# The second layer's residual and two weight roundings change from GpSimd to VectorE

## The chip, the cores and the metric

The kernel runs on one core of a Trainium2 chip. The metric is the device time of one execution in microseconds (us). The engines are TensorE (PE: matmuls and transposes), VectorE (DVE), ScalarE (ACT), GpSimd (POOL) and SyncE (SP, which issues most DMAs). Each engine works through its own list of instructions in order, and an instruction waits on semaphores for what the other engines have to finish first. About 0.2% (2.3 us) is what a measurement of this kernel can tell from no change.

## The reference, cut to what matters

256 latent tokens and 256 context tokens of width 1024 go through a block of two layers (layer A: windowed attention; layer B: neighbourhood attention with a bias), then through a second block (dilated attention and a convolution, then a mixture of 32 experts). All is float32. The change touches the seam between the layers and the end of layer B:

```python
for i in range(DEPTH):                       # DEPTH = 2
    u = h * (1.0 + scale[:, None, :]) + shift[:, None, :]
    uc = hc * (1.0 + scale_c) + shift_c
    ...
    y, yc = mixer(u, uc, w_in, w_out, ...)
    h = layer_norm(DEEPNORM_ALPHA * h + gate[:, None, :] * y, ln_g[i], ln_b[i])
```

`layer_norm` is (x - mean) / deviation, times `ln_g`, plus `ln_b`. The kernel needs the normalized latents twice: as `u` for layer B's projections, and times `ln_g` plus `ln_b` (both multiplied by ALPHA beforehand) as the residual `h1` that is added to layer B's output much later.

## The kernel before, in words

**Products from pairs.** A float32 product is made from three TensorE products: each operand is split into a high half (`hi`, rounded by ScalarE) and a low half (`lo` = value - `hi`). For weights this is `wsplit` (L157 to L177): ScalarE casts 128x2048 in two pieces of 128x1024 (L170), and the subtraction (L175) is shared: the first `cut` of eight rows of 256 go to VectorE in pieces of up to four rows, the others to GpSimd in one piece. `cut` is 5 here, so VectorE gets 128x1024 and 128x256 of each chunk of 256 columns and GpSimd 128x768. For the input of layer B it is `to_u` (L655 to L673): TensorE transposes the tokens (L664), ScalarE makes scaled and shifted `ubhi` (L667), VectorE the same value `uf` (L671), and `ublo` is their difference (L673), on GpSimd for the context tokens and on VectorE for the latents. These differences are the tap roundings of the change's name.

**Between the layers.** `out_a` multiplies layer A's output with four chunks of 256 columns of its weight, adds it to the tokens (`xt`), gathers their statistics, and after the last chunk (`c == 3`) normalizes them in place (L653) and calls `to_u`, first for the context (t = 2, 3), then for the latents (t = 0, 1). Then come the four operations of the residual, on GpSimd: `xt` times `lng` (L723) and plus `lnb` (L724), 128x1024 each. `lng`, `lnb` and `xt` lie in a pool, `o1`, that ends there; the rooms of layer B take its place, so whatever is first written there waits for the last reader.

**Layer B.** For each of four groups G of heads: K into `KS` (`k_stack`: ScalarE casts at L742, VectorE differences at L744), V (ScalarE copies at L794, one for the context, one for the latents), Q (L729 to L735), the gate, then two attentions (m = 0, 1): scores (L835), bias and maximum on VectorE (L839), exponential on ScalarE (L278), division on VectorE (L284), transposes (L843), values (L849), gate (`og`, L852). The projections accumulate in three PSUM banks that all go by the name `mm` and are used in turn. Ahead of the last attention (G = 3, m = 1) the kernel splits weight chunks of layer B's output and of the next block's input; chunks 34 and 35 lie in the rooms of `ubhi` and `ublo`, which have no further use, and `cut = 0` gives their low halves wholly to GpSimd, 128x2048 each. After it come the output product (`osum`, L757) and its statistics (L867).

**Order.** A scheduler lists the instructions of each engine; it works by its own estimate of durations, and keeps the source's order only inside `tc.manual_schedule` for the engines named there. The line numbers after the change are those of before plus three to four, so L742 and L794 become L746 and L798, L839 becomes L841.

Of the kernel before, what the change touches and what calls it, by code (L numbers as in the profile page):

```python
# [13 lines left out]
OP = mybir.AluOpType  # L14
# [6 lines left out]
KT = 8  # L21
# [40 lines left out]
class Net:  # L62
# [621 lines left out]
    def out_a(self, ubp, ogp):  # L684
        tc, nc, d = self.tc, self.nc, self.d
        gr = self.row[0]
        self.ubhi = ubp.tile([P, KT, 512], F32R, name="ubhi")
        self.ublo = ubp.tile([P, KT, 512], F32R, name="ublo")
        sh, sc = self.mod["a", 0], self.mod["a", 1]
        fm = ubp.tile([P, 40], F32, name="fma")  # L690
        nc.sync.dma_start(fm, d["fmv"][:, :40])
        self.gn1 = fm[:, 32:40]
        ab = [self.mod_ab(ubp, fm[:, 0:8], fm[:, 16:24], sc[:, r], sh[:, r], f"mb{r}") for r in range(2)]
        with tc.tile_pool(name="o1", bufs=1, side="right") as o1:
            gates = [self.row_tile(o1, gr[0], "gate0"), self.gates[1]]
            self.xt[0] = o1.tile([P, 2, D], F32, name="xt")
            nc.scalar.dma_start(self.xt[0], d["xtok"][0:2].rearrange("t p d -> p t d"))
            xt = [self.xt[t // 2][:, t % 2, :] for t in range(4)]
            lng = self.row_tile(o1, d["lnrow"][0], "lng")
            lnb = self.row_tile(o1, d["lnrow"][1], "lnb")  # L700
            for r in (lng, lnb):
                nc.gpsimd.tensor_scalar(r, r, ALPHA, 0.0, op0=OP.mult, op1=OP.add)
            st = [o1.tile([P, 4, 6], F32, name=f"st{t}") for t in range(4)]
            ws = dict(enumerate(self.wo))
            for c, ts in ((0, (2, 3)), (1, (2, 3)), (0, (0, 1)), (1, (0, 1)), (2, (2, 3)), (3, (2, 3)), (2, (0, 1)), (3, (0, 1))):
                if c not in ws:
                    ws[c] = self.split("wa_out", c)
                cs = slice(c * 256, c * 256 + 256)
                for t in ts:
                    s = slice(t * P, t * P + P)  # L710
                    if c < 2 and t > 1:
                        y = self.yo[c][:, t - 2]
                        self.mm3(y, self.oparts, ws[c], s, slice(0, 256), range(AOK, KT), 1)
                    else:
                        y = self.ps.tile([P, 256], F32, name="mm", bufs=3)
                        self.mm3(y, self.oparts, ws[c], s, slice(0, 256))
                    self.ln_part(y, gates[t // 2][:, cs], xt[t][:, cs], xt[t][:, cs], st[t], c)
                    if c == 3:
                        self.ln_norm(xt[t], st[t])
                        if t % 2:  # L720
                            self.to_u([xt[t - 1], xt[t]], *ab[t // 2], self.ubhi, self.ublo, P * (t - 1), o1, own=0 if t > 1 else 2)
            for t in range(2):
                nc.gpsimd.tensor_tensor(self.h1[:, t, :], xt[t], lng, op=OP.mult)  # L723
                nc.gpsimd.tensor_tensor(self.h1[:, t, :], self.h1[:, t, :], lnb, op=OP.add)  # L724

    def q_dup(self, ps, qf, QD, scale=0.125):

# [18 lines left out]
    def layer_b(self, ubp):  # L746
        tc, nc, d = self.tc, self.nc, self.d
        u = (self.ubhi, self.ublo)
        lat, ctx, allt = slice(0, 256), slice(256, 512), slice(0, 512)
        with tc.tile_pool(name="b1", bufs=1, side="right") as b1:  # L750
# [3 lines left out]
            def osum(n, last=False):  # L754

                if not last:
                    nc.tensor.matmul(yo[n].rearrange("p i c -> p (i c)"), self.ident, self.h1[:, n // 2, n % 2 * 512:n % 2 * 512 + 512],  # L757
                                     start=True, stop=False, skip_group_check=True)
                for i in range(2):
                    self.mm3(yo[n][:, i], (oghi, oglo), wo[n % 2 * 2 + i], slice(n // 2 * P, n // 2 * P + P), slice(0, 256),  # L760
                             range(BOK, KT) if last else range(BOK), int(last))
# [5 lines left out]
            with tc.tile_pool(name="b2", bufs=1, side="right", reuse_waits="tile") as b2:  # L767
# [6 lines left out]
                for G in range(4):  # L774
# [14 lines left out]
                    for t2 in (1, 0):  # L789
                        ps = self.ps.tile([P, 2, 256], F32, name="mm", bufs=3)  # L790
                        for i in range(2):
                            t = 2 * t2 + i
# [14 lines left out]
                    for m in range(2):  # L807
                        self.filler(f"B{G}{m}")
                        if G == 3 and m == 1:
                            for n, t, b in (("whi", "KS", 4), ("wlo", "vacc", 2)):  # L810
                                self.place[n, 32] = Halves(*(b2.tile([P, 4, 256], F32R, name=t, bufs=b) for _ in range(2)))
                                self.place[n, 33] = Halves(*(self.sp.tile([P, 4, 256], F32R, name="slab", bufs=4) for _ in range(2)))
                            wo = [self.split("wb_out", c) for c in range(2)]
                            self.wsplit(34)
                            wo += self.wsp[32:34]
                            for i, n in ((34, "ubhi"), (35, "ublo")):
                                room = ubp.tile([P, KT, 512], F32R, name=n)
                                self.place["whi", i], self.place["wlo", i] = (room[:, :, j:j + 256] for j in (0, 256))
                            self.cut = 0
                            self.wsplit(36)  # L820
                            self.wn += 2
                            yo = [self.ps.tile([P, 2, 256], F32, name="mm", bufs=3) for _ in range(3)]
                            for n in range(3):
                                osum(n)
                        j = 2 * G + m
                        PT = [None, None]
                        for s in range(2):
                            h = 2 * j + s
                            bt = bias[h % 2]
                            nc.sync.dma_start(bt[:, :, :256], d["bias"][h].rearrange("t p c -> p t c"))  # L830
                            PT[s] = b2.tile([P, 4, 256], F32, name="PT", bufs=3)
                            for qt in range(2):
                                S = self.ps.tile([P, 512], F32, name="s", bufs=2)
                                for part in range(2):
                                    nc.tensor.matmul(S, QD[:, part, s, m, qt * P:qt * P + P], KS[m][:, s, :],  # L835
                                                     start=part == 0, stop=part == 1)
                                st = b2.tile([P, 512], F32, name="st", bufs=4)
                                nm = self.sm.tile([P, 1], F32, name="nm", bufs=6)
                                nc.vector.tensor_tensor_reduce(st, S, bt[:, qt, :], -1.0, BIG, OP.add, OP.min, nm)  # L839
                                self.softmax(st, 512, nm, 0)  # L840
                                pt = self.ps.tile([P, 4, P], F32, name="t", bufs=2)  # L841
                                for kt in range(4):
                                    nc.tensor.transpose(pt[:, kt, :], st[:, kt * P:kt * P + P], self.ident)  # L843
                                nc.scalar.copy(PT[s][:, :, qt * P:qt * P + P], pt)
                        O = self.ps.tile([P, 256], F32, name="o", bufs=1)
                        for kt in range(4):
                            for s in range(2):
                                hh = 2 * m + s
                                nc.tensor.matmul(O[64 * s:64 * s + 64, :], V[:, kt, hh * 64:hh * 64 + 64],  # L849
                                                 PT[s][:, kt, :], start=kt == 0, stop=kt == 3)  # L850
                        og = b2.tile([P, 256], F32, name="og", bufs=1)
                        nc.vector.tensor_tensor(og, O, sg[:, m], op=OP.mult)  # L852
                        nc.scalar.copy(oghi[:, j, :], og)
                        nc.gpsimd.tensor_tensor(oglo[:, j, :], og, oghi[:, j, :].bitcast(F32), op=OP.subtract)
            yo.append(self.ps.tile([P, 2, 256], F32, name="s", bufs=2))
            osum(3)
            with ExitStack() as es:
                b3 = es.enter_context(tc.tile_pool(name="b3", bufs=1, side="right", reuse_waits="tile"))
                lng = self.row_tile(b3, d["lnrow"][2], "lng")
                lnb = self.row_tile(b3, d["lnrow"][3], "lnb")  # L860
# [3 lines left out]
                for n in range(4):  # L864
                    osum(n, True)
                    t, c = divmod(n, 2)
# [832 lines left out]
```

## Time and profile before

| | |
|---|---|
| time, median of 3 runs | 1162.41 us (1161.33 to 1163.54) |
| profiled execution | 1162.07 us |
| its span on the core | 1160.3 us, granted clock 0.979 |
| PE busy | 1072.9 us (92%) |
| DVE busy | 673.6 us (58%) |
| ACT busy | 399.7 us (34%) |
| POOL busy | 144.9 us (12%) |
| DMA | 320.82 MB, mean 276 GB/s |

A share of busy time is a mean over stages that differ. From about 700 us on the experts run behind their weight stream; before that the projections and attentions run, and it is there that the change lies: at 305 to 345 us (end of `out_a`, start of layer B) and 517 to 547 us (last attention). The span is what the records cover; the profiled execution's own time is 1.8 us longer.

### The profile page before, as it was taken

Reading aid. Unit: us, or ns where it says so; the run is one execution under the profiler, and the core shown is the slowest. Engines: PE = TensorE matmul, PEld = TensorE weight load, DVE = VectorE, ACT = ScalarE, POOL = GpSimd, SP = SyncE. Lnnn points to the kernel's source line nnn. Section 1 sums busy time; section 2 is a strip of 40 time slices with the busy share of each in tenths; the row PEclk is TensorE's granted clock in tenths of the full one; section 3 lists DMA queues with packets and bytes.
Section 4 is the critical chain, followed back from the end, with each engine's and each line's share of the span. In section 5 each row is a group of like instructions: output and inputs, shape, how many; then the busy total and the mean of one; then the engine's idle time right before and its main releaser. Section 6 shows DMA issues by size and latency. Waiting matters only on the chain. (4 is left out here: it accounts for less than half of the span.)

```text
span 1160.3 us, 17034 instructions
## 1 busy us (share of the span) xinstructions
PE 1072.9 (92%) x6498; PEld 721.9 (62%) x6499; DVE 673.6 (58%) x1484; ACT 399.7 (34%) x791; POOL 144.9 (12%) x159
## 2 busy tenths in 40 slices
PE   6999999898979999997699898999999998989996
PEld 5777676667978888885689684443434343434432
DVE  3486566886989999895899864332323232322213
ACT  2265462761245645564346652111111010101112
POOL 0141122112442312143200000000000000000000
PEclk9999999999989999999799899999999999999999
DMA  9644528304338887344364787999999999999994
GB/s 364 250 140 152 200 94 285 112 19 141 127 123 310 305 278 264 124 152 149 107 242 154 292 342 273 417 421 420 421 419 422 421 420 421 420 421 421 421 420 173
DMA packets 58840, 320.82 MB, mean 276 GB/s; under 512 B 7001, under 2 KB 11777, under 8 KB 27522
## 3 DMA queue, kind: packets, MB, share of 16 engines
q1 hardware_dynamic: 58338, 318.58, 70.8%
q8 instruction: 53, 0.87, 0.3%
q10 hardware_dynamic: 416, 1.10, 0.3%
q14 instruction: 33, 0.27, 0.1%
HBM read 318.58 MB, written 1.07 MB: 275 GB/s over the span
## 5 line engine op out<-in xcount | busy, mean ns | idle before, releaser
L1433 PE MATMUL U<-ew,XT 128*64 128x512 f32 x512 | 120.8, 595 | 11.9 <-DMA ew<-wu 11.1
L1433 PE MATMUL G<-ew,XT 128*64 128x512 f32 x512 | 117.9, 596 | 4.8 <-DMA ew<-wg 4.7
L175 DVE TENSOR_TENSOR wlo<-raw,whi 128x1024 fp32r<-128x1024 f32 x84 | 100.4, 1218 | 22.4 <-ACT whi L170 22.3
L170 ACT CAST whi<-raw 128x1024 fp32r<-128x1024 f32 x84 | 84.0, 1049 | 82.8 <-PE mm L200 56.2
L1433 PEld LDWEIGHTS U<-ew,XT 128*64 128x64 f32 x512 | 39.4, 137 | 89.0 <-issue 65.3
L175 POOL TENSOR_TENSOR wlo<-raw,whi 128x768 fp32r<-128x768 f32 x32 | 68.3, 2135 | 187.9 <-ACT whi L170 181.7
L1433 PEld LDWEIGHTS G<-ew,XT 128*64 128x64 f32 x512 | 38.7, 137 | 77.5 <-issue 64.8
L278 ACT ACTIVATE st<-st,nm 128x513 f32<-128x513 f32 (+2 forms) x96 | 62.5, 654 | 56.3 <-DVE nm L839 36.2
L1535 DVE SCALAR_TENSOR_TENSOR eth<-eth,U 128x512 f32<-128x512 f32 x16 | 11.0, 688 | 108.8 <-PE U L1433 108.8
L200 PE MATMUL mm<-ublo,whi 128*128 128x256 f32 (+1 forms) x208 | 65.9, 317 | 4.6 <-DVE ublo L673 4.4
L200 PE MATMUL mm<-ubhi,wlo 128*128 128x256 f32 (+1 forms) x208 | 65.5, 315 | 1.3 <-DVE wlo L175 1.3
L228 DVE SCALAR_TENSOR_TENSOR vacc<-slab,stm,vacc 128x1024 f32<-128x1024 f32 x42 | 65.6, 1563 | 0.3
L200 PE MATMUL mm<-ubhi,whi 128*128 128x256 f32 (+1 forms) x208 | 65.4, 316 | 0.0
L1523 DVE SCALAR_TENSOR_TENSOR eth<-eth,G 128x512 f32<-128x512 f32 x16 | 11.0, 688 | 89.2 <-ACT eth L1522 89.2
L1441 ACT COPY hT<-x 128x512 f32<-128x512 f32 x15 | 8.8, 588 | 135.9 <-PE x L1439 135.9
L1452 PE MATMUL Y<-ew,hT 128*64 128x512 f32 x240 | 54.8, 598 | 0.0
L1452 PE MATMUL x<-ew,hT 128*64 128x512 f32 x240 | 54.5, 593 | 0.0
L200 PE MATMUL mm<-uhi,whi 128*128 128x512 f32 x128 | 51.9, 405 | 0.0
L284 DVE TENSOR_SCALAR st<-st,l 128x512 f32<-128x512 f32 (+1 forms) x96 | 50.8, 543 | 1.7
L200 PE MATMUL mm<-ulo,whi 128*128 128x512 f32 x128 | 51.5, 402 | 0.0
L200 PE MATMUL mm<-uhi,wlo 128*128 128x512 f32 x128 | 51.0, 399 | 0.0
L1347 POOL MEMSET ew<- 1x128 f32 x1 | 0.2, 195 | 378.5 <-DMA ew<-wu 378.5
(502 smaller groups left out, 2603.6 us busy)
## 6 DMA issues: line engine op xcount, KB each, us to landing
ew<-wg SPq DMA_DIRECT2D x64, 1024.0 KB, 19.8
ew<-wu SPq DMA_DIRECT2D x64, 1024.0 KB, 19.8
ew<-wd SPq DMA_DIRECT2D x63, 1024.0 KB, 19.8
slab<-wmod SPq DMA_DIRECT2D x48, 512.0 KB, 5.1
slab<-wada SPq DMA_DIRECT2D x32, 512.0 KB, 5.0
raw<-wb_in SPq DMA_DIRECT2D x16, 1024.0 KB, 5.0
raw<-wa_in SPq DMA_DIRECT2D x10, 1024.0 KB, 8.6
raw<-wc_in SPq DMA_DIRECT2D x10, 1024.0 KB, 4.9
```

The lines of the kernel that those rows point to most:

```text
L170: nc.scalar.copy(hi[:, k:k + self.piece[0]], raw[:, k:k + self.piece[0]])
L175: e.tensor_tensor(lo[:, k:to], raw[:, k:to], hi[:, k:to].bitcast(F32), op=OP.subtract)
L200: nc.tensor.matmul(out, a[x][:, k, sa], b[y][:, k, sb], start=(i == 0 and n == 0), stop=(i == len(ks) - 1 and n == 2))
L228: nc.vector.scalar_tensor_tensor(acc, slab, s, acc, op0=OP.mult, op1=OP.add)
L278: nc.scalar.activation(st[:, :width + extra], st[:, :width + extra], AF.Exp, bias=nm, scale=-1.0, accum_out=l[:, 0:1])
L284: nc.vector.tensor_scalar(st[:, :width], st[:, :width], l[:, 1:2], None, op0=OP.mult)
L1347: nc.gpsimd.memset(t[0:1, D:D + P], 1.0)
L1433: nc.tensor.matmul(o[64 * s:64 * s + 64, :], XT[p][k][:, 64 * s:64 * s + 64], self.ew[m, p, k // 4 * 2 + s][:, k % 4, :], start=k == 0, st ...
L1441: nc.scalar.copy(hT, pt)
L1452: nc.tensor.matmul(Y[64 * s:64 * s + 64, :], hT[:, f, 64 * s:64 * s + 64], w, start=f == 0, stop=f == 3)
L1523: nc.vector.scalar_tensor_tensor(th, th, 1.0, G, op0=OP.add, op1=OP.mult)
L1535: nc.vector.scalar_tensor_tensor(th, th, 0.5, U, op0=OP.mult, op1=OP.mult)
```

## The change

The residual moves to VectorE behind `to_u`, and from the last weight chunk of the latents on VectorE keeps the source's order. The low halves of chunks 34 and 35 move from GpSimd, ahead of the last attention in the source, to VectorE in pieces of four rows (`cut = KT`, KT = 8), behind it in the source.

```diff
@@ out_a
+                if c == 3 and 0 in ts:
+                    held = tc.manual_schedule(engines={mybir.EngineType.DVE})
+                    held.__enter__()
                 for t in ts:
...
             for t in range(2):
-                nc.gpsimd.tensor_tensor(self.h1[:, t, :], xt[t], lng, op=OP.mult)
-                nc.gpsimd.tensor_tensor(self.h1[:, t, :], self.h1[:, t, :], lnb, op=OP.add)
+                nc.vector.tensor_tensor(self.h1[:, t, :], xt[t], lng, op=OP.mult)
+                nc.vector.tensor_tensor(self.h1[:, t, :], self.h1[:, t, :], lnb, op=OP.add)
+            held.__exit__(None, None, None)
@@ layer_b
                                 self.place["whi", i], self.place["wlo", i] = (room[:, :, j:j + 256] for j in (0, 256))
-                            self.cut = 0
-                            self.wsplit(36)
                             self.wn += 2
...
                         nc.gpsimd.tensor_tensor(oglo[:, j, :], og, oghi[:, j, :].bitcast(F32), op=OP.subtract)
+            self.cut = KT
+            self.wsplit(36)
             yo.append(self.ps.tile([P, 2, 256], F32, name="s", bufs=2))
```

On VectorE at the end of `out_a`, of the change: the last of `to_u`, the residual (`h`, now L726 and L727), the low half of the Q chunk (`wlo_3416`), and the first sums of a modulation vector (`vacc`).

```order
L671 TENSOR_SCALAR uf<-s,mb_a,mb_c 128x256
L673 TENSOR_TENSOR ublo<-uf,ubhi 128x256
L726 TENSOR_TENSOR h<-xt,lng 128x1024
L727 TENSOR_TENSOR h<-h,lnb 128x1024
L726 TENSOR_TENSOR h<-xt,lng 128x1024
L175 TENSOR_TENSOR wlo_3416<-raw_2923,whi_3415 128x1024
L175 TENSOR_TENSOR wlo_3416<-raw_2923,whi_3415 128x256
L727 TENSOR_TENSOR h<-h,lnb 128x1024
L226 TENSOR_SCALAR vacc<-slab,stm 128x1024
```

Before, L226 followed directly on the last L673; the second L727 now stands six instructions behind it.

On ScalarE at the same place: `ubhi` of the latents, then K's casts, V's copies and the high half of the next chunk.

```order
 L667 ACTIVATE ubhi<-s,mb_c,mb_a 128x256 x2
-L794 ACTIVATE V<-mm 128x512
-L742 CAST KS<-mm 64x512 x2
-L170 CAST whi_3412<-raw_2923 128x1024 x2
-L742 CAST KS<-mm 64x512 x2
-L794 ACTIVATE V<-mm 128x512
-L170 CAST whi_3521<-raw_3301 128x1024 x2
...
+L170 CAST whi_3415<-raw_2923 128x1024 x2
+L746 CAST KS<-mm 64x512 x4
+L798 ACTIVATE V<-mm 128x512 x2
+L170 CAST whi_3524<-raw_3304 128x1024 x2
```

V's first copy (the context's) stood ahead of K's casts and now stands behind all four. The first `KS` lies where `lng` and `lnb` were, so its cast waits for the residual's last reader: L724 on GpSimd before, the second L727 on VectorE now. On TensorE the V product of the latents waits for V's first copy in both, since the copy frees its PSUM bank; the V product of the context stands ahead of the transposes of the latents' second tile now, and was shared out around both before.

On VectorE in the last attention, of the change (before, the rows are the same without the two L175 of `ubhi` and the two of `ublo`, and each L284 of the end follows its own RECIPROCAL):

```order
L284 TENSOR_SCALAR st<-st,l 128x512 x2
L175 TENSOR_TENSOR ubhi<-raw_5399,ubhi 128x4x256 x2
L841 ISA st,nm<-s,bias_3283 128x512
L841 ISA nm 128x1
L841 ISA st,nm<-s,bias_3283 128x512
L841 ISA nm 128x1
L175 TENSOR_TENSOR ublo<-raw_5609,ublo 128x4x256
L841 ISA st,nm<-s,bias_3284 128x512
L841 ISA nm 128x1
L175 TENSOR_TENSOR ublo<-raw_5609,ublo 128x4x256
L841 ISA st,nm<-s,bias_3284 128x512
```

So the scheduler puts the four pieces into the last attention, between its bias operations, though the source has them behind it. GpSimd has neither the residual nor a piece of 128x2048 any more.

## Rows read from the trace of the kernel before

**Rows 1.** Busy time by stretch: stretch, length, then each engine's busy us, PEclk, DMA share, GB/s
```profile
400.00:450.00 50.00, 49.55 (x340) 40.91 (x341) 46.08 (x70) 25.00 (x47) 11.45 (x8) 1.00 0.85 286
...
700.00:1150.00 450.00, 427.81 (x2050) 184.35 (x2051) 125.71 (x298) 61.32 (x109) 0.20 (x1) 1.00 0.97 402
```

**Rows 2.** Timeline of VectorE at the end of out_a: start, us, what, [idle before <-releaser]
```profile
317.35 2.90 DVE L653 TENSOR_SCALAR xt<-xt,mv,rs_y 128x1024 f32<-128x1024 f32 x1
...
322.80 2.48 DVE L673 TENSOR_TENSOR ublo<-uf,ubhi 128x256 fp32r<-128x256 f32 x1
...
328.83 0.53 DVE L671 TENSOR_SCALAR uf<-t,mb_a,mb_c 128x256 f32<-128x256 f32 x1
329.28 0.41 DVE L673 TENSOR_TENSOR ublo<-uf,ubhi 128x256 fp32r<-128x256 f32 x1
329.61 0.99 DVE L671 TENSOR_SCALAR uf<-s,mb_a,mb_c 128x256 f32<-128x256 f32 x2
...
331.52 0.74 DVE L226 TENSOR_SCALAR vacc<-slab,stm 128x1024 f32<-128x1024 f32 x1
```

**Rows 3.** Timeline of GpSimd, the residual of before
```profile
317.32 2.38 POOL L723 TENSOR_TENSOR h<-xt,lng 128x1024 f32<-128x1024 f32 x1 [2.59 <-DVE rs_y L634]
...
322.65 4.85 POOL L724 TENSOR_TENSOR h<-h,lnb 128x1024 f32<-128x1024 f32 x2
```

**Rows 4.** Timeline of TensorE, from K's product of the latents to the first attention
```profile
325.33 0.39 PE L200 MATMUL mm<-ublo,whi 128*128 128x256 f32 x1 [3.23 <-DVE ublo L673]
...
327.84 0.58 PE L200 MATMUL mm<-ublo,whi 128*128 128x256 f32 x1 [1.13 <-DVE ublo L673]
...
334.76 0.28 PE L200 MATMUL mm<-whi,ubhi 128*128 128x256 f32 x1
...
340.45 0.28 PE L200 MATMUL mm<-ubhi,whi 128*128 128x256 f32 x1
...
347.32 0.39 PE L200 MATMUL mm<-ubhi,wlo 128*128 128x256 f32 x1 [0.78 <-DVE wlo L175]
...
355.32 0.73 PE L835 MATMUL s<-KS,QD 128*128 128x512 f32 x2 [0.59 <-DVE QD L735]
```

**Rows 5.** Busy time by stretch around K's product of the latents (columns as in rows 1)
```profile
326.00:328.00 2.00, 0.87 (x5) 0.57 (x4) 2.00 (x3) 0.00 (x0) 2.00 (x3) 0.50 0.00 0
...
332.00:334.00 2.00, 2.00 (x17) 2.00 (x16) 1.93 (x3) 0.00 (x0) 0.00 (x0) 0.87 0.37 61
```

**Rows 6.** Timeline of ScalarE: V's copy of the context, K's casts, V's copy of the latents
```profile
324.39 0.63 ACT L794 ACTIVATE V<-mm 128x512 f32<-128x512 f32 x1
334.77 1.18 ACT L742 CAST KS<-mm 64x512 fp32r<-64x512 f32 x2 [9.75 <-PE mm L200]
...
340.65 0.60 ACT L794 ACTIVATE V<-mm 128x512 f32<-128x512 f32 x1 [1.48 <-PE mm L200]
```

**Rows 7.** Timeline of VectorE: two inputs of 128x1024, alone and beside GpSimd's L175
```profile
337.46 1.23 DVE L175 TENSOR_TENSOR wlo<-raw,whi 128x1024 fp32r<-128x1024 f32 x1
338.60 2.86 DVE L228 SCALAR_TENSOR_TENSOR vacc<-slab,stm,vacc 128x1024 f32<-128x1024 f32 x1
```

**Rows 8.** Timeline of GpSimd in the last attention
```profile
521.11 4.77 POOL L175 TENSOR_TENSOR ubhi<-raw,ubhi 128x2048 fp32r<-128x2048 f32 x1 [0.50 <-ACT ubhi L170]
```

**Rows 9.** Timeline of VectorE in the last attention
```profile
521.01 5.16 DVE L284 TENSOR_SCALAR st<-st,l 128x512 f32<-128x512 f32 x2
...
529.00 0.69 DVE L839 CUSTOM_DVE_ANT_0 st<-s,bias 128x512 f32<-128x512 f32 x1 [1.62 <-PE s L835]
...
533.56 0.49 DVE L284 TENSOR_SCALAR st<-st,l 128x512 f32<-128x512 f32 x1
```

**Rows 10.** Timeline of ScalarE in the last attention
```profile
525.90 2.00 ACT L170 CAST ublo<-raw 128x1024 fp32r<-128x1024 f32 x2 [3.91 <-DMA raw<-wc_in]
```

**Rows 11.** Timeline of TensorE in the last attention
```profile
526.31 0.63 PE L843 MATMUL t<-ident,st 128*128 128x128 f32 x4 [3.36 <-DVE st L284]
...
529.75 1.48 PE L757 MATMUL s<-h,ident 128*128 128x512 f32 x2
```

## The prediction

> **What bounds the kernel now.** I read the busy time by stretch first. From 700 us on the DMA engines are busy 97% of the time, and the experts run behind their weight stream; ahead of it, TensorE is busy 49.55 of 50 us between 400 and 450 [rows 1]. So TensorE sets the pace of layer B, and the stream begins behind the work that TensorE paces: a microsecond that TensorE loses at 305 to 345 us, or in the last attention, moves all that follows. The share of VectorE in that stretch, 46.08 of 50, says that it runs close behind and can't take much more.
>
> Then I read TensorE's timeline for its idle time at the two places of the change. At the end of `out_a` it waits 3.23 and 1.13 us for `ublo` (L673) on VectorE [rows 4]. VectorE is late there because its own instructions are long: one L653 takes 2.90 us and one L673 takes 2.48 [rows 2], while GpSimd works on the residual from 317.32 and again from 322.65 to 327.5 [rows 3]; an undisturbed L673 takes 0.41. Behind these waits the granted clock is 0.50 from 326 on and still 0.87 in 332 to 334 [rows 5], so 1.2 GHz from 327.84 to about 332.5, 4.7 us in which 2.3 us are lost. In the last attention TensorE waits 3.36 us for L284 [rows 11], two of which take 5.16 us [rows 9] beside GpSimd's piece of 128x2048, 4.77 us [rows 8].
>
> **The residual: what is given back.** With GpSimd quiet, `to_u` runs undisturbed: L671 and L673 follow each other every 0.78 us (328.83 to 329.61) [rows 2]. But the V product of the context now stands ahead of the transposes of the second tile. The first tile is normalized at about 317.2 (the next L653 starts at 317.35 [rows 2]); its transposes need 0.8 us (estimated), V's 48 matmuls 5.7 (as the V product of the latents takes from 334.76 to 340.45 [rows 4]). So the second transposes start near 323.7, VectorE's eight pairs near 324, and `to_u` ends at 324 + 8 x 0.78 = 330.2 instead of 331.5. TensorE follows without a long wait and ends K's product of the latents near 330.5, where it ended at 334.76 [rows 4]: 4.3 us gained.
>
> **The residual: what it costs.** The next thing on TensorE is V's product of the latents. It needs the bank that V's first copy frees. That copy was done at 325.0 [rows 6], ahead of K's casts; now it stands behind all four, and the first cast needs the residual's last instruction, whose inputs lie in its room. Step by step on VectorE: `to_u` ends at 330.2; L726, L727, L726 and the piece of 128x1024 take 1.14 each (337.46 to 338.60 [rows 7]), the piece of 128x256 0.4 (as L673 of the same shape [rows 2]), the last L727 1.2: 330.2 + 4.6 + 0.4 + 1.2 = 336.4. The high half that the two pieces need takes ScalarE 2.0 (a cast of the same shape [rows 10]) after K's product ends, 332.5, before VectorE comes to it. At about that time GpSimd has its own part of that chunk; beside such a part an L228 of 128x1024 took 2.86, where the L175 of that size ahead of it took 1.23 [rows 7]. So 0 to 1.6 more; I take 0.6, as the overlap covers only some of these instructions: 337.0. Four casts of 0.59 (1.18 for two [rows 6]) and V's copy of 0.63 follow: 340.0. TensorE starts V's product at 340.0 instead of 334.76, after 9.5 us of idling.
>
> The idle time of 3.23 and 1.13 us was enough for the clock to fall to 0.50 [rows 4, 5]; 9.5 will be too, so I add the 2.3 us again. V's product then ends at 340.0 + 5.7 + 2.3 = 348.0 where it ended at 340.45: 7.5 us late. Behind it are two waits for VectorE, 0.78 and 0.59 [rows 4]. VectorE's own queue is later by 5.5 us (L226 at 337.0 and not 331.52 [rows 2]), less than TensorE, so part of the two goes; I take 0.6 of 1.4. This edit costs 6.9 us, with bounds from 3.3 (no contention, no slow clock, both waits gone: 339.4 + 5.7 - 340.45 - 1.4 = 3.3) to 10 (1.6 of contention, no wait gone, and Q's copy on ScalarE, which now stands behind two more casts of 1.0, adds up to 1.5).
>
> A rule speaks for the edit. The Trainium skill ("GPSIMD Engine Reference", 4.1 Engine selection) says that elementwise work on a tile belongs on VectorE, GpSimd being about two times slower with two inputs. The trace agrees on the ratio: 2.38 us for L723 against 1.23 for a VectorE instruction of the same size [rows 3, 7]. By the rule alone the residual would be 4.8 us shorter and the sum would hold only the gain of 4.3. By the rows its duration isn't what counts: on GpSimd it was over at 327.5, and K's cast waited until 334.77 for TensorE [rows 6]; on VectorE it is over at 337.0.
>
> **The rounding of chunks 34 and 35.** GpSimd's two pieces go, VectorE gets four of 1.2 us. L284 takes its 0.49 again [rows 9], so the wait of 3.36 us goes. What is late next: the high half of chunk 35 waits for a DMA until 525.90 and takes 2.0 [rows 10]. The third bias operation stands behind the first piece of `ublo` now, so it starts at 526.9 + 1.2 = 528.1 and not at 529.00 [rows 9], and the output product, at 529.75 [rows 11], gains 0.9. With shorter idle times ahead of it TensorE may keep its clock for a part; together I take 1.2 us. Bounds: nothing, if the fourth bias operation (behind the second piece, 530.1) holds TensorE as before; 3.4, the whole wait.
>
> **Sum.** +6.9 - 1.2 = +5.7 on the profiled 1162.07, which is 0.3 under the median of 1162.41: 1167.8, and 1168.1 from the median. I say 1168.
>
> **Rivals.**
> - *Faster.* V's copy doesn't bind, so that TensorE goes on with V's product at 330.5. For it: TensorE has three `mm` banks; against it: they are all taken at that point (two halves of K, V of the context). Then the residual gives 4.3 us and the slow clock doesn't return, and with 1.2 from the rounding the time is 1156.6. It turns at the start of V's product: under 334.76 the edit gains. By the rule of engine selection it would be this case.
> - *No change.* VectorE gets through sooner (`to_u` from 323 on, nothing beside GpSimd, V's product at 338.5), the clock recovers at once (-2.3), the two waits vanish (-1.4) and the rounding gives 3.4: 338.5 + 5.7 - 340.45 = +3.8, then +3.8 - 1.4 - 3.4 = -1.0, or up to +1: 1161 to 1163.4. It needs all small terms on one side.
> - *Slower still.* GpSimd's part delays two of the instructions (+1.6), Q's copy adds 1.5, and the rounding gives nothing: about 1172. VectorE at 46 of 50 us [rows 1] makes it likelier than the case before.
>
> A further rule bears on the contention: the Trainium skill ("GPSIMD Engine Reference", 1. Specifications) has GpSimd's SBUF interfaces shared with VectorE, in conflict with VectorE instructions that have two SBUF inputs. All four residual operations have two, so by it they can be held for all of GpSimd's part, and the sum would be the upper end, 1.0 higher; the row of 2.86 us agrees that such a hold exists.
>
> **Chances.** The forecast 0.60, slower still 0.14, no change 0.11, faster 0.15. The forecast alone covers 1165 to 1171. The range has to leave out no more than 2 in 10, so it takes in no change and slower still: 1160 to 1172.5. Against a bound of 0.2%, 2.3 us: slower 0.74, same 0.11, faster 0.15.
>
> **What the profile after would show.** Right: no residual on GpSimd; L653 at 0.8 and L673 at 0.4 us; K's product of the latents over near 330.5; then one idle stretch of TensorE of 8 to 11 us ahead of V's product, released by V's copy on ScalarE, with the granted clock 0.50 behind it; K's four casts directly behind the last L727 at 336 to 338; the stretch 350 to 500 unchanged but shifted by 6 to 8 us; in the last attention L284 at 0.49 and the output product about 0.9 us sooner against the work around it. Wrong: V's product starting before 335, K's casts before L727, or a last attention that gives back as much as the seam loses.

## The result and the profile after

The changed kernel takes 1174.78 us (median of 4 runs, 1170.30 to 1178.55) against 1162.64 for the kernel before on the same chip: a ratio of 1.0113 (95% interval 1.0093 to 1.0133). That is 12.1 us by the medians and 13.1 by the ratio, which is not the quotient of the medians; where it matters below, both are given. The direction and the mechanism were forecast, the size was not: it is twice the +5.7 of the sum, and the time lies above the range of 1160 to 1172.5.

The profiled execution of the change took 1170.30 us, the fastest of its four, so its trace shows less loss than the median. Executions of one kernel differ by a few microseconds early in the program: in this trace all landmarks from 20 to 303 us come 1.0 us sooner than in the trace of before. I add that 1.0 us wherever times of the two are compared, and say "on the scale of before".

The waits of TensorE, longest first, show the new one (engine, line, releaser: us in total, times, longest):

```profile
PE mm L200 <- ACT V L798: 10.0, 1, 10.0
...
PE s L761 <- DVE nm L841: 3.8, 1, 3.8
```

The timeline of TensorE over the same stretch as [rows 4]:

```profile
313.57 0.39 PE L200 MATMUL mm<-ublo,whi 128*128 128x256 f32 x1 [1.67 <-POOL ublo L673]
...
315.38 0.66 PE L664 MATMUL t<-ident,xt 128*128 128x128 f32 x2 [1.07 <-issue]
...
316.97 0.56 PE L200 MATMUL mm<-whi,ubhi 128*128 128x256 f32 x1
...
323.47 0.38 PE L664 MATMUL t<-ident,xt 128*128 128x128 f32 x2
...
326.07 0.39 PE L200 MATMUL mm<-ublo,whi 128*128 128x256 f32 x1 [1.05 <-DVE ublo L673]
...
343.22 0.58 PE L200 MATMUL mm<-whi,ubhi 128*128 128x256 f32 x1 [10.02 <-ACT V L798]
...
351.73 0.28 PE L200 MATMUL mm<-ubhi,whi 128*128 128x256 f32 x1
```

The waits of 3.23 and 1.13 us for `ublo` have become one of 1.05, and ahead of the transposes there are two new short ones of 1.67 and 1.07. V's product of the context runs from 316.97 to 323.47. Then V's product of the latents waits 10.02 us. It starts at 343.22 (344.2 on the scale of before) where it started at 334.76, and is over at 351.73 (352.7) where it was over at 340.45. The timelines of VectorE and then ScalarE show what it waits for:

```profile
325.01 0.54 DVE L671 TENSOR_SCALAR uf<-t,mb_a,mb_c 128x256 f32<-128x256 f32 x1 [5.42 <-ACT ubhi L667]
325.59 0.42 DVE L673 TENSOR_TENSOR ublo<-uf,ubhi 128x256 fp32r<-128x256 f32 x1
325.93 0.54 DVE L671 TENSOR_SCALAR uf<-t,mb_a,mb_c 128x256 f32<-128x256 f32 x1
...
332.32 1.22 DVE L726 TENSOR_TENSOR h<-xt,lng 128x1024 f32<-128x1024 f32 x1
...
335.85 3.16 DVE L175 TENSOR_TENSOR wlo<-raw,whi 128x1024 fp32r<-128x1024 f32 x2
338.93 1.21 DVE L727 TENSOR_TENSOR h<-h,lnb 128x1024 f32<-128x1024 f32 x1
340.07 0.74 DVE L226 TENSOR_SCALAR vacc<-slab,stm 128x1024 f32<-128x1024 f32 x1
```
```profile
340.18 2.37 ACT L746 CAST KS<-mm 64x512 fp32r<-64x512 f32 x4 [5.02 <-DVE h L727]
342.57 0.60 ACT L798 ACTIVATE V<-mm 128x512 f32<-128x512 f32 x1
```

VectorE is undisturbed in `to_u` (0.54 and 0.42 us, against 2.48 in [rows 2]), but it idles 5.42 us ahead of it and comes to L226 at 340.07 (341.1 on the scale of before) instead of 331.52. The four casts follow the last L727 directly, V's copy follows them, and TensorE starts 0.05 us after that copy. By stretch (columns as in [rows 1]) the granted clock is 0.50 behind the two short waits, and again from 336 us on, through the idle time and far into the product:

```profile
316.00:318.00 2.00, 2.00 (x12) 2.00 (x11) 1.72 (x9) 0.00 (x0) 0.00 (x0) 0.50 0.54 225
...
336.00:344.00 8.00, 0.78 (x3) 0.78 (x4) 7.89 (x8) 2.92 (x5) 2.52 (x3) 0.50 0.48 162
...
344.00:346.00 2.00, 2.00 (x12) 2.00 (x11) 1.95 (x3) 0.00 (x0) 0.00 (x0) 0.50 1.05 393
...
348.00:350.00 2.00, 2.00 (x14) 2.00 (x13) 1.66 (x2) 0.00 (x0) 0.00 (x0) 0.67 0.79 274
```

In the last attention TensorE's wait for L284 [rows 11] has given way to one for the third bias operation, which stands behind the first piece of `ublo`; that piece waits for ScalarE's cast, and the cast for a DMA as before. The timelines of ScalarE, VectorE and TensorE, in this order:

```profile
537.67 1.99 ACT L170 CAST ublo<-raw 128x1024 fp32r<-128x1024 f32 x2 [5.02 <-DMA raw<-wc_in]
```
```profile
538.74 1.23 DVE L175 TENSOR_TENSOR ublo<-raw,ublo 128x1024 fp32r<-128x1024 f32 x1 [2.71 <-ACT ublo L170]
539.89 0.68 DVE L841 CUSTOM_DVE_ANT_0 st<-s,bias 128x512 f32<-128x512 f32 x1
```
```profile
540.63 2.07 PE L761 MATMUL s<-h,ident 128*128 128x512 f32 x2 [3.81 <-DVE nm L841]
```

The loss by landmarks of the two traces, on the scale of before: 0 at 303 us; +12.3 at the end of V's product; +11.7 from 400 to 500 us; +13.1 at the `og` of the last attention; +10.8 at the first expert; +9.2 at the end. So the seam between the layers makes the loss.

### The profile page after: what moved, and what is told of

It reads as the page before. It is cut to its first block, busy times and chain, and to the rows that moved or that the text cites. A ratio compares the mean times of both kernels' runs of the same rounds, so it can differ in the third digit from the quotient of the medians.

```text
span 1168.5 us, 17040 instructions
## 1 busy us (share of the span) xinstructions
PE 1070.2 (92%) x6498; PEld 720.4 (62%) x6499; DVE 673.8 (58%) x1492; ACT 399.6 (34%) x791; POOL 125.4 (11%) x153
## 3 DMA queue, kind: packets, MB, share of 16 engines
HBM read 318.58 MB, written 1.07 MB: 274 GB/s over the span
## 5 line engine op out<-in xcount | busy, mean ns | idle before, releaser
L175 DVE TENSOR_TENSOR wlo<-raw,whi 128x1024 fp32r<-128x1024 f32 x84 | 104.6, 1265 | 25.7 <-ACT whi L170 25.7
L175 POOL TENSOR_TENSOR wlo<-raw,whi 128x768 fp32r<-128x768 f32 x32 | 68.1, 2128 | 196.7 <-ACT whi L170 170.0
L228 DVE SCALAR_TENSOR_TENSOR vacc<-slab,stm,vacc 128x1024 f32<-128x1024 f32 x42 | 57.7, 1373 | 1.7 <-DMA slab<-wmod 1.2
L200 PE MATMUL mm<-whi,ubhi 128*128 128x256 f32 x128 | 38.8, 303 | 10.0 <-ACT V L798 10.0
L284 DVE TENSOR_SCALAR st<-st,l 128x512 f32<-128x512 f32 (+1 forms) x96 | 46.3, 495 | 1.5
```

The source lines that it names most:

```text
L175: e.tensor_tensor(lo[:, k:to], raw[:, k:to], hi[:, k:to].bitcast(F32), op=OP.subtract)
L200: nc.tensor.matmul(out, a[x][:, k, sa], b[y][:, k, sb], start=(i == 0 and n == 0), stop=(i == len(ks) - 1 and n == 2))
L228: nc.vector.scalar_tensor_tensor(acc, slab, s, acc, op0=OP.mult, op1=OP.add)
L284: nc.vector.tensor_scalar(st[:, :width], st[:, :width], l[:, 1:2], None, op0=OP.mult)
```

## The experiments

Each ran five rounds against the kernel before on its chip; the ratio is to that.

**1, 2. The two parts apart.** e1 has the residual and the held order, and chunks 34 and 35 as before; e2 has only the roundings on VectorE.

```diff
 e1:  (the diff's hunk in out_a alone)
 e2: -self.cut = 0; self.wsplit(36)   +self.cut = KT; self.wsplit(36)   (behind the last attention)
```

> The residual and the held order alone, chunks 34 and 35 rounded on GpSimd as before. Theory (the seam between the layers makes the whole loss: V's first copy behind K's casts, K's casts behind the last residual instruction): TensorE waits 10 us for V's copy as in the changed kernel, layer B runs 10 to 11 us late, and the time is 8 to 13 us over the kernel before. Rival (the roundings in the last attention make a good part of it, and the scatter): only 5 to 8 us over, with runs within 2.5 us of each other.

> The roundings of chunks 34 and 35 on VectorE alone, the residual on GpSimd as before. Theory: layer B up to the last attention stands as in the kernel before, the last attention changes by -1.2 to +1.4 us, the time is within 2 us of the kernel before. Rival (the roundings cost and scatter): 3 to 6 us over the kernel before, and runs that spread by 5 us or more.

Measured: e1 1.0116 (1.0094 to 1.0138), median 1172.56; e2 1.0026 (1.0010 to 1.0041), 1163.05. The first part is the whole loss, as e1's theory had it. e1's trace has the wait of 10.0 us again. The roundings alone cost some 3 us rather than gaining any, though beside the first part they add nothing that can be told (e4 against e1). In e2 the rival was nearer than the theory: 2.8 us by the medians, 3.0 by the ratio, and runs that spread by 8.9 us (1158.78 to 1167.65), against 6.0 for the kernel before on that chip. Its trace does not show where the time goes: aligned at 303 us, it is 1.9 us late by 500 us, ahead of the roundings, where the unchanged kernel of e8 is 1.4 late too, and 2.8 at the last `og`.

**3. V's copy ahead of K's casts.** For the first group, K's stack is written behind V's first product, so that ScalarE's order is: high half of the Q chunk, V's copy, four casts, V's second copy.

```diff
-                        self.k_stack(ps, KS[m])
+                        if G: self.k_stack(ps, KS[m])
+                        else: kps.append(ps)
...
                         nc.scalar.mul(V[:, 2 * t2:2 * t2 + 2, :], ps, 0.5)
+                        for i, kp in enumerate(kps if t2 else []): self.k_stack(kp, KS[i])
```

> The whole change, but for the first group of heads the code of K's stack is written behind the V product of the context, so that V's first copy stands ahead of K's four casts on ScalarE. Theory: TensorE's wait ahead of V's second product falls from 10.0 to about 2.6 us (it waits for the two casts of the high half, then the copy), the clock stays at its higher level, and Q's product waits about 2 us for K's bank instead: about 8 us faster than the changed kernel, 1164 to 1167. Rival (VectorE's late residual is what costs, by whatever way): TensorE waits just as long one product later, and no more than 3 us are won.

Measured: 1.0103 (1.0082 to 1.0123), median 1171.78. The wait ahead of V's product fell as expected, but hardly anything was won: 1.7 us by the medians, 1.4 by the ratio, against e4 on the same chip. TensorE's timeline:

```profile
337.50 0.58 PE L200 MATMUL mm<-whi,ubhi 128*128 128x256 f32 x1 [2.51 <-ACT V L801]
...
345.52 0.36 PE L200 MATMUL mm<-ubhi,whi 128*128 128x256 f32 x1 [0.66 <-DVE KS L748]
...
357.19 0.58 PE L200 MATMUL mm<-ubhi,wlo 128*128 128x256 f32 x1 [5.50 <-DVE wlo L175]
```

The gate's product now waits 5.50 us for its low half, which stands on VectorE behind four L228 and a late queue. And the clock did not stay up; it is at 0.50 behind the wait of 2.51 as behind that of 5.50:

```profile
338.00:340.00 2.00, 2.00 (x11) 2.00 (x11) 2.00 (x1) 0.00 (x0) 2.00 (x3) 0.50 0.03 8
356.00:358.00 2.00, 0.81 (x4) 0.81 (x4) 2.00 (x2) 0.47 (x1) 0.06 (x1) 0.50 0.81 315
```

My theory that V's copy is the one thing that costs fell here. The stated rival (VectorE's late residual costs by whatever way) held.

**4. The change again.**

> The changed kernel once more, for a second trace and for the spread of its runs beside the others on the same chip. Theory: median 1172 to 1176, the wait of 10 us again, and a spread of several us that does not come from this wait (which the order fixes) but from the stretch of the weight stream. Rival: the wait or the clock at the seam differs between executions by several us.

Measured: 1.0115 (1.0093 to 1.0136), median 1173.45, 1171.06 to 1174.46. The wait is 10.0 us again, and from 303 to 503 us the trace loses 11.8 us against that of before (11.7 in the first one). Between these two traces of the change the spread does not come from the weight stream as I had thought: their executions differ by 3.15 us, and 3.0 of them are there at 303 us (this trace is 1.1 us behind that of before at 23 us and 4.0 at 227). In e1 the stretch behind the last attention differs too: there 14.3 of the 14.7 us lost at the last `og` are left at the end, in the first trace of the change 9.2 of 13.1.

**5, 6, 7. Order, and place of the residual.** e5 keeps the held order but leaves the residual on GpSimd; e6 has the residual on VectorE without the held order; e7 holds the order and writes the residual ahead of `to_u`. All three leave out the roundings.

```diff
 (each against e1)
 e5: -nc.vector.tensor_tensor(self.h1...)       +nc.gpsimd.tensor_tensor(self.h1...)
 e6: -held = tc.manual_schedule(...); held.__enter__()   -held.__exit__(...)
 e7:                          self.ln_norm(xt[t], st[t])
+                             if t < 2:  (the two residual operations of tile t; those behind to_u go)
```

> VectorE's held order alone: the residual stays on GpSimd, chunks 34 and 35 as before. As in the changed kernel, the V product of the context stands ahead of the second tile's transposes, so VectorE idles about 5.4 us ahead of to_u, and its pairs alternate (0.91 us each). ScalarE has V's first copy ahead of K's casts again. Theory (what costs is VectorE's queue, made late by the four residual instructions behind to_u, wherever TensorE then waits): to_u ends at most 1 us later than before, TensorE goes from K's to V's product without a wait, the time is within 2.5 us of the kernel before. Rival (the held order by itself, with its idle 5.4 us, makes the loss): 4 to 8 us over the kernel before.

> The residual on VectorE without the held order; the scheduler then puts its four instructions between and directly behind the two L653, ahead of to_u, and leaves TensorE's order nearly as before. Chunks 34 and 35 as before. Theory: the residual takes about 4.8 us on VectorE, of which some 3 us come before to_u can begin; GpSimd's contention (5.4 us on VectorE before) is gone; to_u ends about 2 us sooner than before and the time is 1 to 4 us under the kernel before. Rival (residual work on VectorE costs its full 4.8 us wherever it stands): 2 to 5 us over the kernel before.

> The held order as in the change, with the residual on VectorE, but written directly behind each tile's L653 and so ahead of to_u, where VectorE idled 5.4 us in the changed kernel. Chunks 34 and 35 as before. Theory: the residual disappears in that idle time, V's first copy stands ahead of K's casts again, TensorE's wait of 10 us goes, the time is within 2 us of the kernel before and some 12 us under the changed one. Rival (held order or residual on VectorE costs by itself): 4 us or more over the kernel before.

Measured: e5 1.0025 (1.0013 to 1.0036), median 1163.62; e6 0.9990 (0.9975 to 1.0004), 1160.84; e7 1.0031 (1.0017 to 1.0046), 1164.22. e5 and e7 came out between their theories and their rivals: 2.9 and 3.6 us by the ratio, where 2.5 and 2 were the most that the theories allowed and 4 the least of the rivals. e6's 1.2 us under can't be told from nothing. So of the 13 us about 3 belong to the held order, and about 10 to the residual standing behind `to_u`: the same four instructions on the same engine cost nothing that can be measured ahead of it (e7 against e5 with the held order, e6 without). In e5 and e7 TensorE goes from K's to V's product without a wait. TensorE's timeline of e7 has a new wait for VectorE's sums behind the gate, where the kernel before waited 0.59 [rows 4]:

```profile
355.80 1.08 PE L235 MATMUL mm<-vacc,ones 128*32 128x256 f32 x8 [2.54 <-DVE vacc L228]
```

e6 takes GpSimd's contention out of `to_u`, and gives it back: its VectorE runs the residual from 317.41 on and begins `to_u` at 322.81 (321.89 before, in that trace), and TensorE idles 3.62 us there. Its timeline of VectorE:

```profile
321.66 1.22 DVE L724 TENSOR_TENSOR h<-h,lnb 128x1024 f32<-128x1024 f32 x1
322.81 0.99 DVE L671 TENSOR_SCALAR uf<-t,mb_a,mb_c 128x256 f32<-128x256 f32 x2
```

The Trainium skill ("GPSIMD Engine Reference", 4.1 Engine selection) puts elementwise work on VectorE. By the rows it is faster there, 1.22 us against 2.38 [rows 3]; by the time it made no difference at best.

**8. The kernel before against itself.**

> The kernel before once more, against itself, for a second trace and for what a difference means: all theories expect a ratio of 1 within 0.2%, and runs that spread by about 5 us; the traces of two executions are to show in which stretches this spread lies (the start, up to 50 us, and 200 to 230 us, going by the offsets between the traces so far), with less than 1 us of it in the last attention.

Measured: 0.9997 (0.9983 to 1.0012), 1157.54 to 1164.46. Its trace is 1.0 us ahead of the first one at 20 us, 2.6 at 303 and 1.1 at 500. So single traces agree to some 2 us only, and the seam takes part in the spread. The stretch of 200 to 230 us that I had named makes only 0.1 us of it, that of 250 to 280 makes 1.7.

**9. Late without the wait.** e7 with four more VectorE instructions behind `to_u`.

```diff
+            for t in range(2):
+                for _ in range(2):
+                    nc.vector.tensor_tensor(self.h1[:, t, :], self.h1[:, t, :], self.h1[:, t, :], op=OP.max)
```

> The kernel of the last but one experiment (residual written ahead of to_u, held order) with four more VectorE instructions of 128x1024 behind to_u that replace h1 by the larger of h1 and h1, so they change no value, read neither lng nor lnb, and nobody waits for them soon. VectorE is as loaded behind to_u as in the changed kernel, but K's casts wait for TensorE alone. Theory of VectorE's queue (the 4.8 us are lost wherever the wait then shows): 4 to 5 us over that experiment, so 7 to 9 over the kernel before. Theory of the chain (last residual instruction, K's casts, V's copy, idle TensorE, low clock): within 2 us of that experiment, 3 to 5 over the kernel before.

Measured: 1.0109 (1.0092 to 1.0126), median 1172.76: 9 us over e7 by the ratios, for 4.8 us of work, more than either theory had, but of the kind that the theory of VectorE's queue had. No cast waits for them. TensorE's timeline shows where they come out:

```profile
353.96 0.73 PE L842 MATMUL s<-KS,QD 128*128 128x512 f32 x2
360.19 1.22 PE L842 MATMUL s<-KS,QD 128*128 128x512 f32 x2 [5.50 <-DVE QD L742]
365.04 2.04 PE L842 MATMUL s<-KS,QD 128*128 128x512 f32 x4 [3.63 <-DVE nm L846]
```

Two waits for VectorE's queue, 5.50 and 3.63 us, now in the first attention, and again a clock of 0.50 behind them. So lateness of VectorE is enough for the loss.

**10. The change with less on VectorE.**

```diff
                 for G in range(4):
+                    self.cut = 5 if G else 2
```

> The changed kernel, but for the weight chunks split during the first group of heads VectorE takes two of the eight rows of the low half instead of five, and GpSimd six. Theory of VectorE's queue: VectorE has some 3 us less to do by the first attention, the time falls by 2 to 3 us against the changed kernel, to 10 to 11 over the kernel before. Theory of the chain: the wait ahead of V's second product falls by 0.9 us only (the piece ahead of the last residual instruction is shorter), and the time by about 1 us.

Measured: 1.0163 (1.0147 to 1.0179), median 1179.81, 5 to 6 us slower than the change. Neither theory had this. VectorE's smaller piece takes longer than the larger one did, since it lies beside GpSimd's larger one, and so does even an instruction of 128x1 in the statistics (L631) beside the chunk ahead of it; the timelines of VectorE, then of GpSimd:

```profile
311.86 3.24 DVE L631 SCALAR_TENSOR_TENSOR rs_t<-rs_y,rs_a 128x1 f32<-128x1 f32 x1
...
339.60 3.90 DVE L175 TENSOR_TENSOR wlo<-raw,whi 128x512 fp32r<-128x512 f32 x1
...
358.01 0.69 DVE L175 TENSOR_TENSOR wlo<-raw,whi 128x512 fp32r<-128x512 f32 x1
```
```profile
311.64 3.44 POOL L175 TENSOR_TENSOR wlo<-raw,whi 128x1536 fp32r<-128x1536 f32 x1
...
339.04 3.92 POOL L175 TENSOR_TENSOR wlo<-raw,whi 128x1536 fp32r<-128x1536 f32 x1 [23.27 <-ACT whi L170]
```

The same L175 takes 0.69 alone and 3.90 beside GpSimd, and ends 0.5 us behind GpSimd's; L631 takes 3.24, where the change has 0.22 for it alone and 1.22 beside GpSimd's 128x768, and ends with GpSimd's. From 303 us to V's product of the latents e10's trace loses 3.2 us against the change's: 0.9 by the time the first transposes start, 1.5 because V's product of the context runs longer at the clock of 0.50, and only 0.75 in the wait ahead of V's product of the latents (10.77 for 10.02), where the last L727 ends at 344.6. The rest came later. The experiment can't tell its two theories apart, as it added contention.

**11. The change without the held order.**

```diff
-                if c == 3 and 0 in ts:
-                    held = tc.manual_schedule(engines={mybir.EngineType.DVE})
-                    held.__enter__()
...
-            held.__exit__(None, None, None)
```

> The changed kernel without the held order: residual on VectorE where the scheduler puts it (ahead of to_u), roundings of chunks 34 and 35 on VectorE. Theory (only the residual's place behind to_u makes the loss): the residual gives -1 us as alone, the roundings 0 to +3, so 1 us under to 2 over the kernel before. Rival (the two parts of the change act on each other): 4 us or more over the kernel before.

Measured: 1.0000 (0.9982 to 1.0017), median 1162.47. The loss is gone with the order, as the theory had it, and nothing shows that the two parts act on each other. Since the scheduler then puts the residual ahead of `to_u`, order and place changed together here; e7 has kept them apart.

**12, 13, 14. Load taken from VectorE.** VectorE has no slack in layer B's first group; the kernel before, by stretch:

```profile
340.00:360.00 20.00, 18.10 (x131) 15.64 (x130) 19.73 (x18) 10.33 (x14) 6.81 (x4) 1.00 0.79 281
360.00:380.00 20.00, 20.00 (x124) 17.54 (x123) 19.70 (x34) 10.48 (x21) 1.85 (x1) 1.00 0.86 302
380.00:400.00 20.00, 20.00 (x164) 18.31 (x165) 20.00 (x31) 12.29 (x21) 7.01 (x4) 1.00 0.86 294
```

VectorE is busy 59.4 of 60 us. The three kernels (before, the change, e3) get a short L228:

```diff
+                w = 64 if st is self.stm else 1024
-                nc.vector.scalar_tensor_tensor(acc, slab, s, acc, ...)
+                nc.vector.scalar_tensor_tensor(acc[:, :w], slab[:, :w], s, acc[:, :w], ...)
```

> The kernel before, with less VectorE work in layer B: of the sums for the second block's modulation vectors (L228 of wmod) only 64 of 1024 columns are added, so those values are left out; their loads stay. It is the base for the next two. VectorE is busy 19.7 to 20.0 of 20 us from 340 to 400 in the kernel before; here about 13 to 15. Expected by both theories: the short waits of TensorE for VectorE at 345 to 357 go, 1 to 4 us under the kernel before.

> The changed kernel with the same relief. Theory (two limits side by side: the chain by K's casts and V's copy on TensorE, and VectorE's full queue behind it, either of which alone loses some 10 us): the chain is still there, TensorE waits 10 us for V's copy, 9 to 12 us over the relieved kernel before. Rival (VectorE's full queue alone): no more than 4 over it.

> The changed kernel with V's copy ahead of K's casts, with the same relief: neither the chain nor the full queue is left. Theory of two limits: TensorE waits about 2.5 us for V's copy, and not for the low half of the gate's chunk; 1 to 5 us over the relieved kernel before, where the same kernel without the relief lost 12. Rival (VectorE's load in 340 to 400 plays no part): 9 us or more over the relieved kernel before.

Measured: e12 0.9979 (0.9965 to 0.9993), median 1157.48, as expected and without the short waits of TensorE; e13 1.0054 (1.0037 to 1.0070), 1167.57; e14 1.0047 (1.0027 to 1.0068), 1166.30. The change loses 10.1 us over the relieved kernel before by the medians, 8.7 by the ratios: near the 9 to 12 of the theory of two limits, and far over the 4 of its rival. Against the 12 to 13 us without the relief, VectorE's load makes only 2 to 5 of them. The wait is there, though in e13's trace it ends with VectorE's difference of the first `KS`, behind the same casts, and not with V's copy. TensorE's timeline of e13:

```profile
344.70 0.55 PE L200 MATMUL mm<-whi,ubhi 128*128 128x256 f32 x1 [9.72 <-DVE KS L749]
```

With V's copy first the loss is still 8.8 by the medians, 7.9 by the ratios, between the 1 to 5 of the theory and the 9 of its rival. TensorE's timeline and VectorE's of e14, an execution of 1162.09 us and so 4 under its median, show why:

```profile
336.38 0.56 PE L200 MATMUL mm<-whi,ubhi 128*128 128x256 f32 x1 [2.50 <-ACT V L802]
...
353.10 0.39 PE L200 MATMUL mm<-ubhi,wlo 128*128 128x256 f32 x1 [2.89 <-DVE wlo L175]
```
```profile
347.78 0.64 DVE L229 SCALAR_TENSOR_TENSOR vacc<-slab,stm,vacc 128x64 f32<-128x64 f32 x1 [2.46 <-DMA slab<-wmod]
...
351.62 0.28 DVE L229 SCALAR_TENSOR_TENSOR vacc<-slab,stm,vacc 128x64 f32<-128x64 f32 x1 [1.00 <-DMA slab<-wmod]
351.82 3.19 DVE L175 TENSOR_TENSOR wlo<-raw,whi 128x1024 fp32r<-128x1024 f32 x2
```

VectorE is no longer full (39.0 of 60 us from 340 to 400), but the gate's low half stands behind four L229 that wait for slabs, and the slabs are issued late: SyncE has them behind a weight load that needs the Q chunk's late low half on VectorE. SyncE's timeline:

```profile
313.43 26.68 SPq L154 DMA_DIRECT2D raw<-wb_in  x2
...
341.54 14.50 SPq L223 DMA_DIRECT2D slab<-wmod  x9
```

So there is a third way from VectorE's lateness to TensorE, through SyncE's queue, and the clock (0.54 in 338 to 340, 0.50 in 354 to 356) again turns each wait of 2.5 to 2.9 us into 4 to 4.5.

## Why the prediction was wrong

**Right.** The new wait stands where it was forecast, of the forecast length (10.0 against 9.5), for the forecast reason: last L727, four casts, V's copy, then TensorE 0.05 us later; the granted clock is 0.50 behind it. That the length fits is in part luck: both its ends came late, 334.1 for 330.5 and 344.2 for 340.0. The gain on L653 and L673 is there, 0.81 and 0.42. That the loss then passes on unchanged to the last attention holds (+12.3 at 352, +11.7 at 500).

**The step that failed: "`to_u` ends at 330.2", and with it "4.3 us gained".** On the scale of before `to_u` ends at 333.3, and K's product at 334.1 instead of 334.76: TensorE gained 0.6 us and not 4.3. The contention did go, and the eight pairs took 7.3 us instead of 9.6; but the new order let them begin 4.1 us later than before, so `to_u` ended 1.8 us later and not 1.3 sooner. TensorE still gained a little, as it followed at a granted clock of 1.00 (326 to 334 us), where it had 0.50 before [rows 5]. Of the 3.1 us between 330.2 and 333.3, 2.0 are its start (326.0, not 324): V's product of the context took 6.5 us and not 5.7, its first part at the lower clock behind the short waits of 1.67 and 1.07 (0.50 in 316 to 318), and L671 waited for ScalarE's `ubhi`, 1.5 us behind the transposes, and not for the transposes. The other 1.1 are the pairs: 0.91 us each (325.01 to 325.93), where each L673 needs the L671 just ahead of it. The rows I had taken alternate too, at 0.78 a pair ([rows 2], 328.83 to 329.61), but by count that L673 is the fifth of its kind and the L671 ahead of it the sixth, so it probably had its input already; no run tests this.

**Two smaller terms.** From the end of `to_u` to L226 I had 6.8, measured 7.75 (332.32 to 340.07): the two pieces of L175 took 3.16 beside GpSimd's and not 1.55, so the contention was 1.6, the upper end, and not 0.6. The Trainium skill ("GPSIMD Engine Reference", 1. Specifications) states this contention for instructions with two SBUF inputs. The traces agree that there is one, here and in e10 (3.90 against 0.69). The slow clock cost 2.8 (V's product 8.5 us against 5.7), not 2.3. The part of later waits that goes, 0.6, was right. In all the residual's edit cost 11.7 in this trace where the sum had 6.9: 3.1 + 0.95 + 0.15 (casts and copy) + 0.5 make 4.7 of the 4.8. It also lies above the upper bound of 10, since the bounds varied the contention, the waits, the slow clock and Q's copy, but not the end of `to_u`.

**The roundings** were given 1.2 us. L284 did recover, and the wait of 3.36 went; but the third bias operation came no sooner (539.89 less the 10.7 us by which the whole stretch is late in this trace is 529.2, against 529.00 before and 528.1 forecast), since the DMA that the cast waits for landed 1.1 us later. Alone they cost 3 us, in the change nothing that can be told from zero; the lower bound of my range for them, no gain, was not low enough.

**What the account of the mechanism lacked.** V's copy was one way of several. Taking it away (e3), taking the room's dependency away (e9), or taking VectorE's load away, alone (e13) or together with it (e14), each left 8 to 13 us, because all are ways by which one late VectorE holds TensorE up. I had read VectorE's load from 400 to 450 us, 46 of 50 [rows 1], and called it close; it is 59.4 of 60 in 340 to 400. With that row the rival "slower still" would have had more weight. The rival of a gain turned on V's product starting before 334.76; it started at 344.2.

**Open.** How the 8.8 us of e14 divide among the late slabs, V's copy behind the casts of the high half, the held order and the clock was not tried: each needs another order of DMAs or casts, which the scheduler sets. Why the roundings cost 3 us alone and none in the change was not settled either. No version that computes the whole beat the kernel before: e6, at 0.9990, is not distinguishable from it.

## What to carry to other kernels

When work moves from a side engine to the end of a busy engine's queue, price the lateness of everything behind it there, not just its duration: 4.9 us of VectorE work cost about 10, and the same work placed where VectorE was waiting anyway cost nothing measurable. Read the load of the receiving engine in the very stretch behind the move, since an engine that is 99% busy there has no idle time in which to catch up; here the load made 2 to 5 of the 13 us. Vary the start of the receiving chain in the bounds too, not only the items behind it. And before you name one wait as the cost, look for the next instruction that the same late engine would hold up, for if there is one, curing the wait only moves it.

## What the runs showed of the hardware

- Two VectorE instructions with two inputs did not end before GpSimd's instruction beside them: one of 128x512 took 3.90 us beside one of 3.92, and 0.69 alone; one of 128x1 took 3.24 beside one of 3.44, and 0.22 alone (e10).
- A single wait of TensorE of 2.5 us was followed by a granted clock of 0.50 to 0.54 (e3, e14), so that V's product took 7.4 to 7.5 us instead of 5.7.
- The kernel before, unchanged, spreads by 7 us on one chip, and its traces differ by up to 2.6 us before layer B begins (e8).
